# Moving the norm's latent column sums behind the fifth context panel, with three partial sums for four, and holding two weight casts behind the last pair

## The chip, the cores and the metric

The kernel runs on one core of one Trainium2 chip. The metric is the device time of one execution in microseconds (us), lower is better. The core has TensorE (PE in the profile, PEld its weight loads), VectorE (DVE), ScalarE (ACT), GpSimd (POOL) and SyncE (SP, which here only issues transfers). Each engine works through its own list of instructions in order; between engines they wait for each other's semaphores.

## The reference

Two layers of a transformer over 512 latent tokens and 256 context tokens of width 1024. In each layer the tokens are normed and modulated, mixed by attention, and then passed through a gated feed-forward part:

```
h_lat = h_lat + g_a * o_lat
h_lat = h_lat + g_f * swiglu(modulate(h_lat, sh_f, sc_f), ffn_w_gate_up[l], ffn_w_down[l])
if ctx_out:                                   # layer 0 alone
    h_ctx = h_ctx + cg_a * o_ctx
    h_ctx = h_ctx + cg_f * swiglu(modulate(h_ctx, csh_f, csc_f), ...)
...
def rms_norm(x):  return x * rsqrt(mean(x * x, axis=-1) + EPS)
def modulate(x, shift, scale):  return rms_norm(x) * (1 + scale) + shift
def swiglu(h, w_gate_up, w_down):
    g, u = split(h @ w_gate_up);  return (silu(g) * u) @ w_down
```

Layer 1 begins with `modulate` of the new `h_lat` and `h_ctx` and a projection of both (queries, keys, values). The case is about the seam between the two: the end of layer 0's feed-forward part, the norm that opens layer 1, and the first three projections.

## The kernel before

**Layout.** Activations lie transposed: 1024 features are 8 tiles (`k` or `m`, 0 to 7) of 128 partitions, tokens run along the free dimension, 512 latent columns (`LATS`) and then 256 context columns (`CTXS`). A float32 product is made of three reduced-precision matmuls: an operand is cast to a high part (`wh`, on ACT) and a low rest (`wl`, on DVE), and `mm3` multiplies high by high, high by low and low by high.

**Who sets the order.** The kernel is written in one Python program; a scheduler of the build, with a timeline of its own, then chooses the order on each engine. The call `behind(ins, *before)` adds a dependency for that scheduler alone, with no semaphore: the named instructions must stand earlier on their engine.

**The last pair of layer 0's feed-forward.** A `Pair` makes one block of 128 hidden features: `head`, `body` and `tail` each run products on PE (lines 1386 to 1388) into banks `z` and `y`. In the last step of `body`, ACT copies `z` out of PSUM (line 1436) and DVE adds `y` to it (line 1437); then `tail` goes on adding into `z`, so PE's next product waits for that ACT copy. Up to this point SP has been loading weights in order through three `wr` buffers.

**The last down projection: `output`, called by `final0`.** Its first stream makes the 8 latent panels: for each `m`, matmuls over the two remaining hidden blocks, a residual on DVE (`add_residual`, line 1227), and `norm.add`, which squares the new tile on ACT (line 383) and adds the squares up. Because `norm1` has `two=LATS`, those sums go into separate partial sums: tiles 0 to 3 on POOL, the later ones on DVE. The second stream makes the 8 context panels (256 columns each) in the same manner, with the norm of the latent columns laced in: `rest` first calls `rstd`, which sums the squares over partitions by matmuls of the partial sums against a column of ones (line 397; one per 128 tokens and partial sum), takes the square root (line 400, ACT) and the reciprocal (line 401, DVE), and spreads the result over all partitions by transposes (line 377, `spread`). Then, for each `k`, `modulate` multiplies on DVE (line 432), adds the shift and casts on ACT (line 433) and makes the low rest on DVE (line 434).

**The next weights.** While `final0` runs, `kept_w` loads and casts three weight tiles of layer 1's input projection (keys, values, first queries) at panels 3, 4 and 5: `load_w` casts on ACT (line 334, `wh`) and makes the rest on DVE (line 335, `wl`). The projection itself is at lines 765 to 767.

**PSUM.** `PG` hands out banks in a ring of s, t, s, d, t, s, d with 3 `s`, 2 `t` and 2 `d` banks; a panel waits until the residual of the panel that had its bank is done.

Of the kernel before, what the change touches and what calls it, by code (L numbers as in the profile page):

```python
# [12 lines left out]
ALU = mybir.AluOpType  # L13

P = 128
D = 1024
KT = D // P
# [52 lines left out]
BG = (0, 0, 0, 0, 0)  # L70
LATE = ((0, 1, 3, 5, 7), ()), (0,) * 4 + (1, 2, 2, 2, 1, 2, 2, 2, 1, 2, 3, 2, 1, 2, 3, 2, 0, 0), ((2,), (2,)) + ((0, 2, 4, 6),) * 3
FIRST = 2000
STEPS = ((2, 3, 4, 4), 5, 3)
HALVES = (slice(0, 256), slice(256, 512))
SWAP8 = [(i // 16) * 16 + (i % 16 + 8) % 16 for i in range(32)]
# [24 lines left out]
def hybrid_kernel(ctx: ExitStack, tc, I, out):  # L100
# [6 lines left out]
    def T(tag, shape, dt=F32):  # L107
        count[0] += 1
        if tag not in SIZES:
            return sb.tile(shape, dt, tag=tag, name=f"{tag}_{count[0]}", bufs=BUFS.get(tag, 1))  # L110
        n = int(np.prod(shape[1:]))
        t = sb.tile([P, SIZES[tag] // (2 if dt == mybir.dt.bfloat16 else 4)], dt, tag=tag, name=f"{tag}_{count[0]}",
                    bufs=BUFS[tag])[: shape[0], :n]
        if len(shape) == 3:
            t = t.rearrange("p (a b) -> p a b", a=shape[1])
        return t

    def B(dt=F32, tag="b"):
        return T(tag, [P, NT], dt)
# [12 lines left out]
    V, S, G, PE = nc.vector, nc.scalar, nc.gpsimd, nc.tensor  # L132

    def dma(o, i, eng=None):
        return (eng or nc.sync).dma_start(f(o), f(i))

    def f(ap):
        return ap.bitcast(F32) if ap.dtype == F32R else ap

    silu, marks = [], {}  # L140

    def behind(ins, *before):

        for x in before:
            tc.add_manual_dep(ins.ins, x.ins.name, mybir.DependencyInfo(mybir.DependencyClass.NoSync,
                              mybir.DependencyReason.DATA), reason="products in one run")
        return ins
# [181 lines left out]
    def load_w(src, kt, m, eng=None, tag=None, after=()):  # L329

        r = T("wr", [P, kt * m])
        dma(r, src)
        h, lo = (B(F32R, tag)[:, : kt * m] if tag else T(x, [P, kt * m], F32R) for x in ("wh", "wl"))
        behind(S.copy(h, r), *after[:1])  # L334
        behind((G if eng else V).tensor_tensor(lo, r, f(h), op=ALU.subtract), *after[1:])  # L335
        return tuple(x.rearrange("p (k m) -> p k m", k=kt) for x in (h, lo))
# [14 lines left out]
    def banks(cols, get, rows=P):  # L351

        return [(get()[:rows, : c.stop - c.start], c) for c in cols]
# [32 lines left out]
        marks["add"] = (eng or V).tensor_tensor(acc[:, :n], acc[:, :n], t[:, :n], op=ALU.add)  # L386
        return acc

    def rstd(acc, nfeat, c, r, get=PQ, tag="p"):


        n, accs = c.stop - c.start, [x for x in acc if x is not None] if type(acc) is list else [acc]
        m, d = n // P, get()
        col = T("sm", [P, 6, 2]).rearrange("p a b -> p (a b)")[:, :m]
        for j, a in enumerate(accs):
            for i in range(m):
                x = PE.matmul(d[:, i : i + 1], a[:, i * P : (i + 1) * P], ones[:, :1], start=i + j == 0,
                              stop=j == len(accs) - 1, skip_group_check=True)
                marks["sum"] = behind(x, *([marks["sum"]] if i + j else []))
        marks["root"] = S.activation(col, d[:, :m], AF.Sqrt, bias=eps, scale=1.0 / nfeat)  # L400
        marks["diag"] = V.reciprocal(col, col)
        for i in range(0, n, 512):
            w = min(512, n - i)
            d = get() if r is not None else PS("o")
            for j in range(0, w, P):
                at = (i + j) // P
                marks["spread"] = spread(d[:, j : j + P], col[:, at : at + 1].to_broadcast([P, P]))
            if r is None:
                return d
            S.copy(r[:, c.start + i : c.start + i + w], d[:, :w])  # L410
# [25 lines left out]
    class Norm:  # L436


        def __init__(self, src, use, eng=None, order=range(KT), two=None):
            self.src, self.use, self.eng, self.acc, self.order, self.two, self.marks = src, use, eng, None, order, two, {}  # L440

        def add(self, k, c):
            if c is self.two:
                self.acc = self.acc if k else [None] * 4
                i = (k > 3) + (k > 5) + (k > 6)
                self.acc[i] = square_sum(self.acc[i], self.src[k], c, eng=(G, V)[min(i, 1)])
            else:
                self.acc = square_sum(self.acc if k else None, self.src[k], c, eng=self.eng if k < KT - 1 else None)

        def rest(self, acc, c, v):  # L450
            self.marks[c.start] = own = dict(marks)
            r = Columns(rstd(acc, D, c, None, PG), c.start)
            own.update({x: marks[x] for x in ("sum", "root", "diag", "spread")})
            yield
            for k in self.order:
                self.use(k, r, c, v)
                yield
# [77 lines left out]
    def weighted(o, lanes):  # L535
# [13 lines left out]
        for n in range(max(len(m) for m in moving)):  # L549
            for i, (v, _, all_qs) in [*enumerate(lanes)][::-1]:  # L550
                if n < len(moving[i]):
                    kt, qs, t = moving[i][-1 - n]
                    c = slice((qs[0] - all_qs[0]) * P, (qs[-1] + 1 - all_qs[0]) * P)
                    with shifted(-FIRST):
                        ins = PE.matmul(o[64 * i : 64 * i + 64, c], v(kt), t, start=n == 0, stop=n == len(moving[i]) - 1)  # L555
# [205 lines left out]
    r = B(tag="nb")  # L761
# [120 lines left out]
    acc = None  # L882
    for k in range(KT):
        acc = square_sum(acc, X[k], LATS)
        behind(marks["square"], *silu)
    behind(ident_cast, marks["square"])
    _, diag = first_norm(acc, LATS)
# [8 lines left out]
    for c in range(4):  # L896
# [16 lines left out]
        if c == 3:  # L913
            _, diag = first_norm(acc, CTXS)
# [230 lines left out]
    def na_jobs():  # L1145
        for p in range(4):
            if p == 3:
                lower[0] = L3
            for x in ORDER[p]:
                beside(split_pair(int(x)) if x in "23" else {"n": latent_norms, "m": mla_prepare}[x]())  # L1150
            rate[0] = STEPS[0][p], BG[p]
            if p % 2 == 0:
# [12 lines left out]
    i = 0  # L1165
# [21 lines left out]
    def mla_jobs():  # L1187
        phase[0], lower[0] = 1, LOWER
        rate[0] = STEPS[1], BG[4]
        ready.append(latent_operands(1))  # L1190
# [43 lines left out]
    ahead, soon = {}, []  # L1234

    def kept_w(src, m):

        if 2 < m < 6:
            soon.append(load_w(I["w_in1"][(8, 9, 0)[m - 3]], KT, P))
        return ahead[m]  # L1240

    def keep_groups(k0, kc):
# [12 lines left out]
    def output(src, mov, l, comp, streams, norm, units, dst=None, keep=False, base=None, wait=0, held=()):  # L1255

        rest, kept, done = iter(()), [], []
        for i, (c, v) in enumerate(streams):
            if i and norm.two:
                next(rest)  # L1260
                own = norm.marks[streams[0][0].start]
            before = done[-1:] + ([marks["add"]] if i and norm.two else [])
            for m in range(KT):
                w = kept[m] if keep and i else keep(src, m) if callable(keep) else load_w(src(m), len(mov), P, LOE[l, comp, i], "b" if keep else None, held[m : m + 1] * 2 if i == 0 else ())
                if keep and i == 0:
                    kept.append(w)
                o = banks([c], PG)
                ins = mm3(o, w, mov)
                if i and norm.two:
                    behind(ins, *(own[x] for x in {2: ("sum",), 4: ("spread",)}.get(m, ())))  # L1270
                    before = before + [own["diag"]] if m == 2 else before
                done.append(behind(add_residual(m, o[0][0], l, comp, v, c, dst and dst[m], base and base(m, c)), *before))
                if c is TOK1:
                    G.dma_start(home[m], H[m])
                norm.add(m, c)
                if i and norm.two:
                    behind(marks["square"], own["root"])
                if m >= wait:
                    next(rest, None)
                if m in units[i]:  # L1280
                    late_step(done[-1], m < 7)
            for _ in rest:
                pass
            rest = norm.rest(norm.acc, c, v)
        for _ in rest:
            pass
# [90 lines left out]
    norm, ops, sums = combined(H, 0, 3, TOK1, TOK2)  # L1377
# [12 lines left out]
    class Pair:  # L1390
# [39 lines left out]
        def body(self):  # L1430
            self.y = PG()[:, : self.w]
            product(self.z, self.s2, self.ops["T2"])
            S.copy(self.t[:, self.c1], self.z)
            product(self.y, self.s3, self.ops["T3"], True)
            product(self.z, self.s1, self.ops["T1"])
            S.copy(self.t[:, self.c2], self.z)  # L1436
            self.done = V.tensor_tensor(self.t[:, self.c2], self.y, self.t[:, self.c2], op=ALU.add)

        def tail(self):
            product(self.z, self.s4, self.ops["22"])  # L1440
# [187 lines left out]
    lower[0] = LOWER  # L1628
    rate[0] = STEPS[2], 0
    attend(swa_jobs())  # L1630
# [7 lines left out]
    norm, ops, sums = combined(H, 1, 3, *HALVES)  # L1638
# [178 lines left out]
```

## Time and profile before

| what | value |
|---|---|
| time, median of 3 runs | 1577.79 us (1577.0, 1577.79, 1583.72) |
| the profiled execution | 1578.6 us, its span 1576.6 us |
| TensorE busy in the span | 1530.6 us (97%) |
| VectorE, ScalarE, GpSimd busy | 1174.0, 794.5, 276.0 us |
| mean granted TensorE clock | 0.992 |
| the seam, in us of the span | last pair 940 to 961, latent panels to 971, context panels and norm 971 to 986, projections from 986 |

The span reaches from the first to the last instruction; the execution's own time is 2.0 us more. A row of the timeline reads: start, duration, engine, line, operation, output<-inputs, sizes, count, and in brackets the idle time of the engine just before, with what ended it. A row of the windows gives the busy time of each engine in a stretch, then the granted TensorE clock (1.00 is full speed), the share of the DMA engines in use and GB/s. Line numbers in the profile of before are those of the kernel before; the kernel after has 1 to 4 lines more, so that line 397 is 398 there, and 1436 is 1440.

### The profile page before, as it was taken

How to read it: one execution, taken by the hardware profiler on the slowest of the kernel's cores; microseconds unless marked ns; L12 is line 12 of the kernel's file. 1: busy time of each engine (PE TensorE's matmuls, PEld its weight loads, DVE VectorE, ACT ScalarE, POOL GpSimd, SP SyncE). 2: the span in 40 equal slices, each digit the busy share in tenths (PEclk: the TensorE clock that was granted, in tenths of full speed). 3: DMA queues.
4: the chain of work that ended last, by engine and by line, in shares of the span. 5: the costliest groups of instructions: out<-in, count | busy, mean ns of one | idle time of the engine just before them, and what ended most of it. 6: DMA issues, size and time to landing. Idle time of an engine off the chain costs nothing.

```text
span 1576.6 us, 26539 instructions
## 1 busy us (share of the span) xinstructions
PE 1530.6 (97%) x10024; PEld 1375.8 (87%) x10024; DVE 1174.0 (74%) x2345; ACT 794.5 (50%) x1607; POOL 276.0 (18%) x302
## 2 busy tenths in 40 slices
PE   6999999999999999999999999999999999999998
PEld 4787778887998999999999998877889999899998
DVE  4885777685878587777858675889976778678685
ACT  4563677775465243242423334548856545454453
POOL 0144624320111101102111131470012000000001
PEclk9999999999999999999999999999999999999999
DMA  9644242004654444646466494110125123323222
GB/s 317 250 131 175 78 129 73 11 7 160 207 168 143 154 165 161 219 134 264 157 202 236 146 351 145 49 46 2 68 78 164 52 98 126 98 90 128 86 96 87
DMA packets 76463, 214.90 MB, mean 136 GB/s; under 512 B 9872, under 2 KB 16400, under 8 KB 76336
## 3 DMA queue, kind: packets, MB, share of 16 engines
q1 hardware_dynamic: 59216, 144.42, 27.6%
q0 software_dynamic: 15968, 67.24, 12.3%
q8 instruction: 78, 1.28, 0.3%
q10 hardware_dynamic: 1152, 1.57, 0.3%
q14 instruction: 49, 0.40, 0.1%
HBM read 186.97 MB, written 23.07 MB: 133 GB/s over the span
## 4 chain that ended last, share of the span: by engine, by line
PE 79%; DVE 9%; DMA 5%; ACT 3%; issue 2%; POOL 1%; SPq 0%; DVEq 0%; ACTq 0%; POOLq 0%
PE pss L1388 5%; PE pss L1387 5%; PE pss L1386 5%; PE pso L555 4%; PE pss L345 4%; PE psd L345 4%; PE pss L348 4%; PE pss L347 4%; PE psd L348 4%; PE psd L347 4%; PE pst L345 3%; PE pst L1388 3%; PE pst L1386 3%; PE pst L348 3%; PE pst L347 3%; PE pst L1387 3%
## 5 line engine op out<-in xcount | busy, mean ns | idle before, releaser
L334 ACT CAST wh<-wr 128x1024 fp32r<-128x1024 f32 (+2 forms) x148 | 115.5, 795 | 210.9 <-DMA wr<-in_w_dn_dram 42.1
L335 DVE TENSOR_TENSOR wl<-wr,wh 128x1024 fp32r<-128x1024 f32 (+2 forms) x145 | 133.9, 930 | 81.7 <-ACT wh L334 81.5
L561 ACT ACTIVATE p<-p,sm 128x512 f32<-128x512 f32 (+3 forms) x144 | 105.0, 730 | 29.0 <-DVE sm L565 27.2
L1386 PE MATMUL pss<-b,wh 128*128 128x384 f32 (+1 forms) x346 | 107.8, 312 | 0.6 <-ACT b L371 0.6
L1387 PE MATMUL pss<-b,wh 128*128 128x384 f32 (+1 forms) x346 | 108.0, 312 | 0.1
L1388 PE MATMUL pss<-b,wl 128*128 128x384 f32 (+1 forms) x346 | 107.2, 312 | 0.0
L347 PE MATMUL psd<-b,wh 128*128 128x512 f32 (+3 forms) x262 | 89.7, 343 | 0.0
L301 DVE CUSTOM_DVE_ANT_0 p<-rope,cond 128x1024 bf16<-128x1024 f32 x64 | 76.9, 1221 | 11.0 <-DMA rope<-in_mod_w_dram 10.8
L291 POOL DMA_DIRECT2D rope<-in_mod_w_dram x48 | 25.6, 533 | 318.7 <-DVE mod L301 306.0
L345 PE MATMUL psd<-b,wh 128*128 128x512 f32 (+3 forms) x222 | 80.0, 360 | 1.2 <-ACT b L474 0.9
L348 PE MATMUL psd<-b,wl 128*128 128x512 f32 (+3 forms) x222 | 78.8, 356 | 0.0
L555 PE MATMUL pso<-ph,b 128*64 128x256 f32 (+1 forms) x384 | 77.5, 361 | 0.4 <-DVE ph L500 0.2
L555 PE MATMUL pso<-pl,b 128*64 128x256 f32 (+1 forms) x384 | 77.2, 359 | 0.0
L1386 PE MATMUL pst<-b,wh 128*128 128x384 f32 (+1 forms) x226 | 70.8, 313 | 3.1 <-ACT p L1436 1.8
L1373 ACT CAST wh<-pl 128x512 fp32r<-128x512 f32 x78 | 44.9, 619 | 52.0 <-PE pss L1387 22.8
L1388 PE MATMUL pst<-b,wl 128*128 128x384 f32 (+1 forms) x226 | 70.7, 313 | 0.2 <-DVE wl L1374 0.2
L1387 PE MATMUL pst<-b,wh 128*128 128x384 f32 (+1 forms) x226 | 70.6, 312 | 0.0
L347 PE MATMUL pss<-b,wh 128*128 128x256 f32 (+3 forms) x216 | 69.3, 321 | 0.0
L1373 ACT CAST wh<-wr 128x1024 fp32r<-128x1024 f32 x39 | 41.0, 1051 | 54.4 <-PE pst L1387 14.7
L345 PE MATMUL pss<-st,wh 128*128 128x512 f32 (+2 forms) x198 | 67.2, 339 | 0.3 <-ACT wh L334 0.3
L348 PE MATMUL pss<-st,wl 128*128 128x512 f32 (+2 forms) x198 | 67.3, 340 | 0.1
L1386 PEld LDWEIGHTS pss<-b,wh 128*128 128x128 f32 x346 | 65.7, 190 | 1.1 <-ACT b L371 0.9
(624 smaller groups left out, 5387.4 us busy)
## 6 DMA issues: line engine op xcount, KB each, us to landing
wr<-in_w_gu_dram SPq DMA_DIRECT2D x88, 512.0 KB, 4.1
rope<-in_mod_w_dram POOLq DMA_DIRECT2D x48, 512.0 KB, 3.9
wr<-in_w_dn_dram SPq DMA_DIRECT2D x73, 256.0 KB, 2.9
wr<-in_w_out_dram SPq DMA_DIRECT2D x32, 512.0 KB, 4.2
p<-home POOLq DMA_DIRECT2D x40, 384.0 KB, 5.5
home<-p POOLq DMA_DIRECT2D x40, 384.0 KB, 5.4
wr<-in_w_in_dram SPq DMA_DIRECT2D x21, 512.0 KB, 3.8
nb<-in_nb_dram SPq DMA_DIRECT2D x16, 384.0 KB, 3.3
```

Of the source, the lines that this page charges most:

```text
L301: behind(V.tensor_tensor_reduce(out=T("p", [P, D], mybir.dt.bfloat16), in0=w, in1=cond[:, v, :], op0=ALU.mult, op1=ALU.add, scale=1.0, sca ...
L334: behind(S.copy(h, r), *after[:1])
L335: behind((G if eng else V).tensor_tensor(lo, r, f(h), op=ALU.subtract), *after[1:])
L345: ins = PE.matmul(o, wh[:, k], mh[:, c], start=first and k == 0, stop=False)
L347: PE.matmul(o, wh[:, k], ml[:, c], start=False, stop=False)
L348: PE.matmul(o, wl[:, k], mh[:, c], start=False, stop=last and k == n - 1)
L555: ins = PE.matmul(o[64 * i : 64 * i + 64, c], v(kt), t, start=n == 0, stop=n == len(moving[i]) - 1)
L561: S.activation(p[:, c], p[:, c], AF.Exp, bias=nm, scale=-1.0, accum_out=dn)
L1373: S.copy(h, t)
L1386: PE.matmul(o, wh, xh, start=first and k == 0, stop=False, skip_group_check=not first)
L1387: PE.matmul(o, wh, xl, start=False, stop=False, skip_group_check=not first)
L1388: PE.matmul(o, wl, xh, start=False, stop=k == 3, skip_group_check=not first)
```

## The change

Three edits. `norm1` keeps three partial sums of the latent squares and not four: tile 7 is added to the sum of tile 6 on DVE. The column sums, which stood behind the first context panel, are written in ahead of the sixth (`m == 5`) and held behind the fifth panel's first matmul; the sixth panel is held behind the sums, the seventh (`m == 6`) behind the spread, and the squares of the context tiles 5 to 7 behind the root. And of the three next weight tiles, the second and third are cast (and their rests made) only behind the last DVE step of the last pair's `body`, which `marks["middle"]` names.

```diff
+SUMS = 5, 6
...
-    def rstd(acc, nfeat, c, r, get=PQ, tag="p"):
+    def rstd(acc, nfeat, c, r, get=PQ, tag="p", after=()):
...
-                marks["sum"] = behind(x, *([marks["sum"]] if i + j else []))
+                marks["sum"] = behind(x, *([marks["sum"]] if i + j else after))
...
-                self.acc = self.acc if k else [None] * 4
-                i = (k > 3) + (k > 5) + (k > 6)
+                self.acc = self.acc if k else [None] * 3
+                i = (k > 3) + (k > 5)
...
-            r = Columns(rstd(acc, D, c, None, PG), c.start)
+            r = Columns(rstd(acc, D, c, None, PG, after=self.hold), c.start)
...
-            soon.append(load_w(I["w_in1"][(8, 9, 0)[m - 3]], KT, P))
+            soon.append(load_w(I["w_in1"][(8, 9, 0)[m - 3]], KT, P, after=(marks["middle"],) * (m > 3)))
...
-            if i and norm.two:
-                next(rest)
-                own = norm.marks[streams[0][0].start]
+            late = i and norm.two
...
+                if late and m == SUMS[0]:
+                    norm.hold = ins,
+                    next(rest)
+                    norm.hold, own = (), norm.marks[streams[0][0].start]
+                    before = before + [own["diag"]]
                 o = banks([c], PG)
                 ins = mm3(o, w, mov)
-                if i and norm.two:
-                    behind(ins, *(own[x] for x in {2: ("sum",), 4: ("spread",)}.get(m, ())))
-                    before = before + [own["diag"]] if m == 2 else before
+                if late and m in SUMS:
+                    behind(ins, own[("sum", "spread")[SUMS.index(m)]])
...
-                if i and norm.two:
+                if late and m >= SUMS[0]:
                     behind(marks["square"], own["root"])
-                if m >= wait:
+                if m >= (SUMS[0] if late else wait):
...
-            self.done = V.tensor_tensor(self.t[:, self.c2], self.y, self.t[:, self.c2], op=ALU.add)
+            self.done = marks["middle"] = V.tensor_tensor(self.t[:, self.c2], self.y, self.t[:, self.c2], op=ALU.add)
```

**TensorE, the context panels.** A panel is six matmuls of 128x256; `st` are the two hidden blocks, `nb` and `st_97..` the weights, `ones` by `p_9864`, `p_9919` and so on the column sums of the partial sums, `ident_r` by `sm` the spread. Before, from the last matmul of the first context panel on:

```order
L348 MATMUL psd_9983<-st_9645,nb_9744 128x256
L397 MATMUL pss_9958<-ones_93,p_9864 128x1 x4
L397 MATMUL pss_9958<-ones_93,p_9919 128x1 x4
L397 MATMUL pss_9958<-ones_93,p_9946 128x1 x4
L397 MATMUL pss_9958<-ones_93,p_9956 128x1 x4
L345 MATMUL pss_9993<-st_9540,nb_9743 128x256
...
L348 MATMUL pst_10061<-st_9540,st_9750 128x256
L377 MATMUL pso_9978<-ident_r_86,sm_9959 128x128 x4
L345 MATMUL psd_10044<-st_9540,st_9749 128x256
```

After, from the last matmul of the fifth context panel on:

```order
L349 MATMUL pss_10002<-st_9645,st_9750 128x256
L398 MATMUL psd_10013<-ones_93,p_9864 128x1 x4
L398 MATMUL psd_10013<-ones_93,p_9919 128x1 x4
L398 MATMUL psd_10013<-ones_93,p_9946 128x1 x4
L346 MATMUL pst_10034<-st_9540,st_9749 128x256
...
L349 MATMUL psd_10068<-st_9645,st_9756 128x256
L378 MATMUL pso_10029<-ident_r_86,sm_10014 128x128 x4
L346 MATMUL pss_10051<-st_9540,st_9755 128x256
...
L767 MATMUL pst_10189<-b_10045,wh_9890 128x512
```

The sums move from behind panel 1 of 8 to behind panel 5 and fall from 16 matmuls to 12; between sums and spread stood three and a half panels (21 matmuls) and now stand two (12), and between the spread and the first projection three and a half and now one.

**ScalarE, the last pair.** `p_9680<-pst_9681` is the copy of the last pair's bank `z`, the `CAST` of `wh` those of the next weights. Before:

```order
L1373 CAST st_9755<-wr_9754 128x512
L334 CAST wh_9907<-wr_9905 128x1024
L1436 COPY p_9680<-pst_9681 128x384
L1373 CAST st_9540<-p_9574 128x384
L334 CAST wh_9923<-wr_9921 128x1024
L1441 ACTIVATE p_9679<-pst_9681 128x384
```

After:

```order
L1377 CAST st_9755<-wr_9754 128x512
L1440 COPY p_9680<-pst_9681 128x384
L1377 CAST st_9540<-p_9574 128x384
L335 CAST wh_9907<-wr_9905 128x1024
L335 CAST wh_9923<-wr_9921 128x1024
L1445 ACTIVATE p_9679<-pst_9681 128x384
```

The copy that PE waits for now stands ahead of the cast of the values' weights; the cast of the queries' weights keeps its place ahead of the silu.

**ScalarE, the root.** `p<-b ... 128x256` are squares of context tiles, the `ACT_TABLE_LOAD` belongs to the square root. Before:

```order
L383 ACTIVATE p_9956<-b_9839 128x512
L400 ACT_TABLE_LOAD
L400 ACTIVATE sm_9959<-pss_9958,eps_91 128x4
L383 ACTIVATE p_9991<-b_9832 128x256
L383 ACTIVATE p_10001<-b_9833 128x256
```

After:

```order
L384 ACTIVATE p_9956<-b_9839 128x512
L384 ACTIVATE p_9967<-b_9832 128x256
L384 ACTIVATE p_9977<-b_9833 128x256
L384 ACTIVATE p_9988<-b_9834 128x256
L384 ACTIVATE p_9999<-b_9835 128x256
L384 ACTIVATE p_10010<-b_9836 128x256
L401 ACT_TABLE_LOAD
L401 ACTIVATE sm_10014<-psd_10013,eps_91 128x4
L384 ACTIVATE p_10042<-b_9837 128x256
```

Five context squares now stand ahead of the table load and the root; behind it comes the sixth.

On DVE the order changes in the same way: the fourth partial sum becomes one more addition (`p_9946<-p_9946,p_9956`) ahead of the first context residual, and the reciprocal stands behind the fifth context residual and not behind the first. On SP, the transfers `parked` (the latent result to memory, held behind the root for the scheduler) now stand behind the load of a mask that used to follow them. Outside the seam only the first scores of layer 1's attention stand in a slightly other order on PE and DVE.

More of the change, by code (lines that the diff above doesn't have):

```diff
@@ L440, in __init__ @@
             self.src, self.use, self.eng, self.acc, self.order, self.two, self.marks = src, use, eng, None, order, two, {}
+            self.hold = ()
         def add(self, k, c):
             if c is self.two:
-                self.acc = self.acc if k else [None] * 4
-                i = (k > 3) + (k > 5) + (k > 6)
+                self.acc = self.acc if k else [None] * 3
+                i = (k > 3) + (k > 5)
                 self.acc[i] = square_sum(self.acc[i], self.src[k], c, eng=(G, V)[min(i, 1)])
```

## The prediction

> **What bounds the kernel.** I read the page first, then the windows around the seam, then what PE waited for there, then the timeline of each engine in it.
>
> ```profile
> span 1576.6 us, 26539 instructions
> PE 79%; DVE 9%; DMA 5%; ACT 3%; issue 2%; POOL 1%; SPq 0%; DVEq 0%; ACTq 0%; POOLq 0%
> ```
>
> The chain that ended last runs through PE for 79% of the span, so time is won where PE stands still or runs slowly. The windows by stage (last pair, latent panels, context panels and norm, projections, then the way into attention) show where that is:
>
> ```profile
> 940.00:955.00 15.00, 14.06 (x82) 13.74 (x80) 7.66 (x13) 6.97 (x12) 2.14 (x4) 1.00 0.71 251
> 955.00:971.00 16.00, 15.19 (x72) 13.30 (x73) 9.71 (x15) 6.56 (x12) 1.56 (x2) 1.00 0.45 160
> 971.00:986.00 15.00, 13.53 (x88) 13.19 (x86) 7.54 (x14) 7.03 (x14) 4.50 (x5) 0.77 0.33 120
> 986.00:1004.00 18.00, 17.57 (x80) 14.02 (x79) 14.19 (x29) 8.10 (x17) 2.40 (x3) 1.00 0.01 1
> 1004.00:1014.00 10.00, 10.00 (x70) 9.22 (x69) 7.33 (x12) 4.32 (x9) 7.96 (x6) 1.00 0.15 52
> 1014.00:1032.00 18.00, 18.00 (x87) 15.10 (x86) 17.52 (x24) 11.57 (x17) 13.33 (x8) 1.00 0.33 117
> ```
>
> From 971 to 986 PE is idle for 1.5 us and its granted clock is 0.77; from 1004 to 1032 it never stops, so what PE wins before 1004 has nothing there that would swallow it. What PE waited for between 940 and 1070:
>
> ```profile
> PE pst L1386 <- ACT p L1436: 1.8, 1, 1.8
> PE pss L397 <- POOL p L386: 1.5, 1, 1.5
> PE pss L755 <- DVE sm L565: 1.1, 1, 1.1
> ...
> PE pst L766 <- DVE b L434: 0.4, 1, 0.4
> ```
>
> The change aims at the first two; the fourth it can only worsen.
>
> **The last pair.** PE's two rows and ACT's three:
>
> ```profile
> 953.73 0.34 PE L1388 MATMUL pst<-b,wl 128*128 128x384 f32 x1
> 955.82 0.44 PE L1386 MATMUL pst<-b,wh 128*128 128x384 f32 x1 [1.75 <-ACT p L1436]
> ```
>
> ```profile
> 954.34 1.04 ACT L334 CAST wh<-wr 128x1024 fp32r<-128x1024 f32 x1 [1.35 <-DMA wr<-in_w_in_dram]
> 955.29 0.47 ACT L1436 COPY p<-pst 128x384 f32<-128x384 f32 x1
> ...
> 958.10 1.05 ACT L334 CAST wh<-wr 128x1024 fp32r<-128x1024 f32 x1 [1.92 <-PE pst L1387]
> ```
>
> PE's product ends at 954.07. ACT is then casting a weight for which it had stood idle 1.35 us, and copies only at 955.29. With the copy ahead, it starts at about 954.1, so PE restarts at 954.65 in place of 955.82: -1.2 us. Bounds: 0 if ACT is late anyhow, -1.75 if the whole wait went. I take -1.2, since every part of it is in these rows. What now queues behind the copy: the values' cast (about 955.1 to 956.1), then the queries' cast, which may stay at 958.1 if it is its own transfer and not PE that ends last, and behind it the silu that stood at 959. A silu that comes no earlier is harmless: PE reads that pair's products in its second half of the latent panels, some 5 us later. The two casts and their DVE rests are read by the projections, from 985.7; that cover is 26 us long, and the cost is nothing. `middle` adds no semaphore, and the order shows that the edit does what it says.
>
> **The sums.** PE around them:
>
> ```profile
> 971.67 0.28 PE L348 MATMUL psd<-st,nb 128*128 128x256 f32 x1
> 973.42 5.63 PE L397 MATMUL pss<-ones,p 128*128 128x1 f32 x32 [1.48 <-POOL p L386]
> ...
> 979.49 0.42 PE L348 MATMUL pss<-st,nb 128*128 128x256 f32 x1
> 979.70 0.41 PE L345 MATMUL pss<-st,nb 128*128 128x256 f32 x1
> ...
> 981.82 0.28 PE L347 MATMUL pss<-st,st 128*128 128x256 f32 x1
> 981.93 0.28 PE L348 MATMUL pss<-st,st 128*128 128x256 f32 x1
> ```
>
> First, the wait of 1.48 us. After, four more panels stand ahead of the sums: 4 x 6 x 0.12 (the step from 981.82 to 981.93) = 2.9 us, so PE reaches them at about 974.7 by the old clock, when POOL has long ended. -1.5 us.
>
> Second, the sums themselves: 16 matmuls in two passes are 32 rows in 5.63 us; 12 will be 24. The price of a row depends on the clock:
>
> ```profile
> 974.00:974.50 0.50, 0.50 (x7) 0.50 (x6) 0.31 (x1) 0.50 (x1) 0.00 (x0) 1.00 0.99 377
> 974.50:975.00 0.50, 0.50 (x6) 0.50 (x5) 0.00 (x0) 0.08 (x1) 0.00 (x0) 0.94 1.02 385
> 975.00:975.50 0.50, 0.50 (x4) 0.50 (x4) 0.00 (x0) 0.00 (x0) 0.00 (x0) 0.50 0.72 270
> ...
> 981.50:982.00 0.50, 0.50 (x5) 0.50 (x5) 0.14 (x1) 0.07 (x1) 0.35 (x1) 0.73 0.00 0
> ```
>
> The grant falls to half at about 974.97 and comes back at 981.8: most of the sums and the twelve matmuls behind them run at half clock. At full clock the same kind of row is priced by the final norm:
>
> ```profile
> 1556.57 1.84 PE L1658 MATMUL psd<-ones,p 128*128 128x1 f32 x16
> ```
>
> 0.115 us each, so 24 cost 2.8 us: -2.9 us. Bounds: at the old mean of 0.176 they cost 4.2 (-1.4); at 0.115 it is -2.9.
>
> Third, the twelve slow matmuls at 0.21 (979.49 to 979.70) in place of 0.12: -1.1 us if the clock holds, 0 if not.
>
> Does it hold? Before 974.97 PE had streamed real columns only until 971.9; 1.5 us of idling and 1.5 of one-column rows followed, and the clock fell. The 1.75 us idle at 954 did not make it fall (1.00 in both windows there). After, the run of one-column rows is 2.8 us with full panels on both sides: between the two, nearer to the one that fell. [...]
>
> By rows alone: let the clock be judged over stretches of 3.4 us (half of the dip from 974.97 to 981.8), and let a fall need 2.4 us without real columns in one of them (halfway between 1.75 and 3.0). A run of 2.8 us then meets it at (0.6 + 2 x 0.4) / 3.4, some 4 in 10 positions. I take "holds" for the sum and the fall as a rival.
>
> **What the move adds.** The rows of the chain from sums to the first projection, ACT and DVE, and the spread and first projections on PE:
>
> ```profile
> 973.30 1.28 ACT L400 ACT_TABLE_LOAD   x1
> 979.09 0.26 ACT L400 ACTIVATE sm<-pss,eps 128x4 f32<-128x4 f32 x1 [4.51 <-PE pss L397]
> ...
> 984.18 1.38 ACT L433 ACTIVATE b<-p,mod 128x512 fp32r<-128x512 f32 x2 [0.64 <-DVE p L432]
> 985.47 0.71 ACT L383 ACTIVATE p<-b 128x256 f32<-128x256 f32 x2
> ```
>
> ```profile
> 972.47 1.45 DVE L386 TENSOR_TENSOR p<-p,p 128x512 f32<-128x512 f32 x1
> 973.84 0.47 DVE L1227 SCALAR_TENSOR_TENSOR b<-psd,mod,b 128x256 f32<-128x256 f32 x1
> 979.39 0.18 DVE L401 RECIPROCAL sm<-sm 128x4 f32<-128x4 f32 x1 [5.08 <-ACT sm L400]
> ...
> 983.40 1.41 DVE L432 SCALAR_TENSOR_TENSOR p<-b,mod,pso 128x512 f32<-128x512 f32 x2 [0.31 <-PE pso L377]
> ```
>
> ```profile
> 982.76 0.60 PE L377 MATMUL pso<-ident_r,sm 128*128 128x128 f32 x4
> ...
> 985.71 0.40 PE L765 MATMUL pst<-b,wh 128*128 128x512 f32 x1
> ...
> 988.41 0.50 PE L766 MATMUL pst<-b,wh 128*128 128x512 f32 x1 [0.43 <-DVE b L434]
> ```
>
> The new DVE addition (0.7 to 1.45 us by the row at 972.47) starts at 973.84 and ends by 975.3; PE needs it after 16 rows of sums, at 976.5. Hidden.
>
> The root now stands behind five context squares and the table load. The context residuals start behind that addition, say at 974.6, and step by 0.4; the fifth ends at 976.6, its square at 977.05, the table load (1.28) at 978.35. The sums end at 974.7 + 2.8 = 977.5, so the load, once hidden, is late by 0.9 us; root and reciprocal bring the column to 978.85. PE has two panels (1.4 us) to pass that time, to 978.9. Cost 0, with no margin: every further tenth costs a tenth. Bounds 0 and +1 (the addition at 1.45, and one more residual late).
>
> From the spread on: DVE's first product starts 0.64 us after the spread does, ACT's cast 1.42 after, and takes 0.7. So PE can project 2.2 us after the spread began and has until then 0.36 of spread and one panel of 0.72: idle 1.1. The low rest (0.74 on DVE) and the second tile, in the new DVE order, cost it another 0.3 and 0.5. Before, three and a half panels covered this, and the waits were 0.43 and 0.12. So +1.4 us; bounds +0.5 (the first idle alone, less the old waits) and +3.
>
> SP: the `parked` transfers queue behind the mask load, which waits for PE's last read of `nb` in the third context panel (973.2). They start 5 us later; nothing reads them before attention is over. POOL has the same rows in the same order. In the first scores of attention PE's order shifts by some rows near the wait of 1.1 us on L565: 0, bounds -1 and +1.
>
> **The sum**, against the profiled execution of 1578.6 us: -1.2 (pair) -1.5 (wait) -2.9 (sums) -1.1 (slow panels) +0 (root) +1.4 (first projection) = -5.3, so 1573.3 us. That execution stands 0.8 above the median of 1577.79, so the gain against the median is 4.5 us, or 0.3%. A change of 0.5%, 7.9 us, is about what a measurement of this kernel can tell from no change: I expect a real gain too small for that.
>
> **The rivals.**
>
> The clock still falls behind the sums. For it: the row at 975.00, and a run of 2.8 us at almost full loads. Then some 3.4 us of panels run at half speed, costing 1.7 less the 0.2 that the idling before the projection absorbs: +1.5, 1574.8 us. Chance 0.30.
>
> The wait moves instead of going: DVE does residuals, modulation and rests in one line, and PE idles 4.5 us before and in the first projections, not 1.9. For it: DVE is busy 14.19 of 18 us there; against it: a tile takes two DVE operations of 0.7 us, and PE waited only 0.43 for them. 1576 us, chance 0.13.
>
> Slower than before: the root. Five squares, each behind a residual behind a panel, stand before it on one in-order engine. If POOL holds the `p` buffers that these squares need, or DVE's addition drags, ACT is late and PE has no further panel to run. Each us is lost in full, and it decides from 5.3 us on; PE would then idle long enough for the clock to fall as well, some 1580 us. Against it: POOL's latent additions end by 973.4. Chance 0.05.
>
> More than I count: attention's first wait of 1.1 us goes too and the copy wins all its 1.75: about 1571.5. Chance 0.10.
>
> **The numbers.** The forecast, clock held, has 0.42: 1573.3 us. The range of 1570.8 to 1577.0 takes in the fall, the larger gain and most of the moved wait. Faster by over 0.5% needs the large gain and more: 0.05; slower by that much: 0.02; the rest, 0.93, is within.
>
> **What would show it.** The copy of `z` starting within 0.1 us of PE's last row of that product; no idle ahead of the ones; 24 rows in 2.8 us with the clock at 1.00; the spread right behind the second panel; an idle of about 1 us ahead of the first L767 row. Wrong would prove a clock of 0.50 behind the sums, a root later than 1 us after them, or waits of over 3 us in the first three tiles of the projection.

## The result, and the profile after

| kernel | median us | runs | ratio to the kernel before, 95% interval |
|---|---|---|---|
| before | 1578.26 (1575.6 to 1586.73) | 17 | |
| after | 1573.63 (1570.5 to 1581.96) | 17 | 0.9968 (0.9956 to 0.9979) |
| after, in a later comparison (before there 1579.78) | 1573.64 (1570.18 to 1575.83) | 6 | 0.9955 (0.9939 to 0.9971) |

A gain of 4.6 us, near the forecast of 1573.3 us and inside its range. The prediction held a gain of 0.3% for too small to tell from none; over 17 runs each it can be told, since the interval ends below 1. The profiled execution of after, however, took 1578.6 us, as long as that of before. So the place of the change must be read by itself. First, what PE waited for between 935 and 1070 us (us in total, times, longest):

```profile
PE pss L757 <- DVE sm L567: 1.2, 1, 1.2
PE pst L767 <- ACT b L434: 1.1, 2, 0.9
PE pst L1392 <- DVE wl L1378: 0.8, 1, 0.8
...
PE pst L1390 <- ACT p L1440: 0.6, 1, 0.6
```

The wait for POOL ahead of the sums is gone, the one for the copy of `z` (line 1440 now) has shrunk from 1.8 to 0.6, and the first projections wait 1.1. The third row stands in the pair before, ahead of everything that the change touches. The timeline of the pair, PE and then ACT:

```profile
957.77 0.34 PE L1392 MATMUL pst<-b,wl 128*128 128x384 f32 x1
958.73 0.44 PE L1390 MATMUL pst<-b,wh 128*128 128x384 f32 x1 [0.62 <-ACT p L1440]
...
958.20 0.48 ACT L1440 COPY p<-pst 128x384 f32<-128x384 f32 x1 [1.17 <-PE pst L1392]
...
958.99 1.05 ACT L335 CAST wh<-wr 128x1024 fp32r<-128x1024 f32 x1
961.21 1.05 ACT L335 CAST wh<-wr 128x1024 fp32r<-128x1024 f32 x1 [1.17 <-DMA wr<-in_w_in_dram]
```

ACT copies 0.09 us behind PE's product, and the casts follow. The sums and what comes behind them, on PE and on ACT and DVE:

```profile
977.56 2.73 PE L398 MATMUL psd<-ones,p 128*128 128x1 f32 x24
...
981.54 0.28 PE L349 MATMUL psd<-st,st 128*128 128x256 f32 x1
981.77 0.65 PE L378 MATMUL pso<-ident_r,sm 128*128 128x128 f32 x4
...
984.01 0.50 PE L767 MATMUL pst<-b,wh 128*128 128x512 f32 x1 [0.88 <-ACT b L434]
...
986.22 0.50 PE L767 MATMUL pst<-b,wh 128*128 128x512 f32 x1 [0.22 <-ACT b L434]
```

```profile
979.95 1.28 ACT L401 ACT_TABLE_LOAD   x1
981.24 0.26 ACT L401 ACTIVATE sm<-psd,eps 128x4 f32<-128x4 f32 x1
...
981.54 0.18 DVE L402 RECIPROCAL sm<-sm 128x4 f32<-128x4 f32 x1 [2.12 <-ACT sm L401]
```

No idle ahead of the ones, 24 rows in 2.73 us, the root's reciprocal ready at 981.72 while the second panel's last matmul runs, and a new wait of 0.88 us, then one of 0.22. The windows of that stretch (the granted clock stands behind the five engines):

```profile
977.50:980.30 2.80, 2.80 (x27) 2.80 (x27) 1.92 (x5) 2.34 (x6) 1.39 (x2) 1.00 0.93 342
980.30:982.30 2.00, 2.00 (x17) 1.85 (x18) 0.76 (x3) 1.37 (x3) 1.53 (x3) 1.00 1.02 379
```

The clock held at 1.00. To compare kernels whatever happens elsewhere, I take the **seam**: from the start of PE's last row of the product that ACT copies (953.73 before, 957.77 after) to the start of ACT's first rope copy out of `psd` (1007.12 and 1005.40). It took 53.4 us before and 47.6 after, a gain of 5.8 us.

Where did that execution lose it? Against the same ACT instructions of before it lay 0.9 us late at 700 us, 1.8 at 840, 3.4 from 850 on and 4.0 at 950; behind the seam it was 1.7 early, and level again from 1075. Two of the losses, some 1.6 us each, show in its windows:

```profile
842.15:845.56 3.41, 1.54 (x10) 1.22 (x9) 3.41 (x7) 1.28 (x2) 0.28 (x1) 1.00 0.10 42
845.56:848.97 3.41, 3.41 (x12) 3.41 (x11) 3.37 (x6) 0.00 (x0) 1.01 (x3) 0.50 0.66 188
...
1053.77:1057.18 3.41, 1.77 (x12) 1.06 (x10) 3.35 (x10) 1.83 (x4) 3.33 (x3) 1.00 0.00 0
1057.18:1060.60 3.42, 3.42 (x18) 2.44 (x20) 3.35 (x10) 1.04 (x3) 0.09 (x1) 0.50 0.00 0
```

Twice PE stood still for half of a stretch of 3.41 us, and in the next 3.41 us its clock was granted at half. In the profile of before the clock stayed at 1.00 at both places, with waits of nearly the same length (1.39 and 1.1 us for 1.87 and 1.23). The first place lies ahead of the change. At the second, in attention, the clock fell in 1 of the 3 profiles with the sums in their old place (the hold alone) and in 4 of the 9 with the sums moved: too few to tell a difference, so the fall there isn't charged to the change, but it isn't shown to be free of it. What the falls went with, the experiments show.

### The profile page after: what moved, and what is told of

Its sections match the earlier page's. It is cut to its first block, busy times and chain, and to the rows that moved or that the text cites. A ratio compares the mean times of both kernels' runs of the same rounds, so it can differ in the third digit from the quotient of the medians.

```text
span 1576.8 us, 26525 instructions
## 1 busy us (share of the span) xinstructions
PE 1529.3 (97%) x10016; PEld 1372.7 (87%) x10016; DVE 1174.8 (75%) x2346; ACT 796.1 (50%) x1607; POOL 276.3 (18%) x302
## 4 chain that ended last, share of the span: by engine, by line
PE 77%; DVE 10%; DMA 6%; ACT 3%; issue 2%; POOL 0%; SPq 0%; DVEq 0%; ACTq 0%; POOLq 0%
PE pso L557 5%; PE pss L1392 5%; PE pss L1391 5%; PE pss L1390 4%; PE psd L346 4%; PE psd L349 4%; PE psd L348 4%; PE pss L346 4%; PE pss L349 4%; PE pss L348 3%; PE pst L1392 3%; PE pst L1390 3%; PE pst L1391 3%; PE pst L346 3%; PE pst L348 3%; PE pst L349 3%
```

## The experiments

All seams, in one table (measured from the start of PE's row as above, also where an expectation speaks of its end): idle time of PE in the pair, idle ahead of and within the sums, rows of one column and their time, length of the half clock that began in or behind them, idle of PE ahead of the spread and in the first two tiles of the projection. Every ratio below is to the kernel before as timed beside that run, whose median was 1579.24 to 1579.78 us.

| kernel | pair | sums | rows, us | half clock | spread; projection | seam |
|---|---|---|---|---|---|---|
| before | 1.75 | 1.48 | 32, 5.63 | 6.83 | 0; 0.43 | 53.4 |
| after, first profile | 0.62 | 0 | 24, 2.73 | none | 0; 0.88, 0.22 | 47.6 |
| after, second | 0.62 | 0 | 24, 3.06 | 6.83 | 0; 0.31, 0.21 | 49.6 |
| after, third | 0.62 | 0 | 24, 2.93 | 3.41 | 0; 0.88, 0.22 | 49.0 |
| hold of the casts alone | 0.62 | 1.49 | 32, 5.74 | 10.24 | 0; 0.45 | 53.6 |
| sums alone | 1.89 | 0 | 24, 2.73 | 3.41 | 0; 0.32, 0.18, 0.22 | 49.7 |
| four partial sums, moved | 0.62 | 0 | 32, 3.63 | 3.41 | 0; 0.32, 0.84 | 49.6 |
| three partial sums, in place | 1.97 | 1.47 | 16 and 8, 1.95 and 1.70 | 6.83 | 0; 0.17, 0.56 | 52.9 |
| two partial sums, early | 0.62 | 0.71 | 16 | none | 0; 0.95, 0.23 | 47.3 |
| two partial sums, moved | 0.62 | 0 | 16, 1.99 | none | 0.50; 0.95, 0.23 | 47.2 |
| fixed order | 0.62 | 0 | 16, 1.99 | none | 0.18; 0.25, 0.82 | 46.8 |
| fixed order, early | 0.62 | 0.71 | 16 | none | 0; 0, 0.39, 0.31 | 46.8 |

**The hold of the casts alone.** Before, with `after=(marks["middle"],) * (m > 3)` in `kept_w` and the mark.

> The old kernel with the second half of the change alone: the last two weight casts held behind the pair's middle, the sums where they were. What is compared in the trace here and below is the seam: from the end of PE's last row of T1 in the last pair to the start of ACT's first copy out of the projected keys (rope, b<-psd), 53.4 us in the old kernel's trace and 47.6 in the new one's. Theory (the terms add up): the wait ahead of the next product falls from 1.75 us to about 0.6, the wait for POOL ahead of the sums stays at 1.5 or grows by what POOL does not gain, the clock still falls behind the sums, and the seam takes 52.2 us; time 1.2 us below the old kernel's. Rival (the copy only moves the wait): PE comes to the sums 1.2 us earlier and waits there 2.7 us for POOL, whose additions hang on the same squares; seam 53.4, time unchanged.

1577.84 us, ratio 0.9984 (0.9959 to 1.0009). The wait in the pair fell to 0.62 us and the wait for POOL stayed at 1.49, so the rival's mechanism is out: POOL gained what PE gained. But the seam is no shorter, because the clock stayed at half for 10.24 us here and not 6.83:

```profile
978.10:979.50 1.40, 1.35 (x12) 1.36 (x13) 0.93 (x2) 1.19 (x1) 0.00 (x0) 1.00 0.96 364
979.50:983.00 3.50, 3.50 (x19) 3.50 (x18) 0.00 (x0) 0.00 (x0) 0.00 (x0) 0.51 0.03 11
983.00:986.40 3.40, 3.40 (x17) 3.40 (x17) 0.66 (x2) 0.98 (x3) 0.00 (x0) 0.50 0.00 0
986.40:989.80 3.40, 3.40 (x18) 3.40 (x17) 1.30 (x3) 0.83 (x3) 2.21 (x3) 0.50 0.19 58
```

The 1.1 us won ahead of the sums went into 0.9 more from the sums to the spread and 0.7 more from there to the projection.

**The sums alone.** After, without that argument.

> The new kernel without the hold of the two casts: the sums moved and three for four, the casts as in the old kernel. Theory (the terms add up): the wait of 1.75 us in the pair is back, everything from the sums on stands as in the new kernel (24 rows in 2.7 to 2.8 us, clock 1.00), seam 48.8 us, time 4.1 us below the old kernel's. Rival (the early copy also makes room for the sums): without it ACT and POOL come later and PE waits ahead of the moved sums as well, seam 50 us or more, and the clock falls.

1574.09 us, ratio 0.9966 (0.9943 to 0.9989). The wait of 1.89 us is back, PE waits nowhere ahead of the sums: the rival is out in that, the parts don't lean on each other. But the clock fell behind the sums, for 3.41 us, with the same 24 rows in the same 2.73 us behind which it had held in the first profile of after. The seam is 0.9 us over the 48.8 expected; I put that down to the fall.

**Four partial sums at the new place.** After, with `[None] * 4` and `i = (k > 3) + (k > 5) + (k > 6)`.

> The new kernel with four partial sums in place of three: 32 rows at the new place. Rows cost 0.115 us at full clock, so 3.7 us. Theory (the clock falls when a window of 3.41 us has under about a third of its time in streaming matmuls): the run now covers up to the whole of a window and the clock falls in some 7 executions of 10; where it falls, the rows cost 0.17 to 0.2 us and twelve to twenty matmuls behind them run at half speed, seam 50 to 51 us; where it does not, 48.5. Rival (only idle time makes the clock fall, and rows of one column count as work): the clock stays at 1.00 and the seam is 48.5, time 0.9 us above the new kernel's.

1574.41 us, ratio 0.9971 (0.9953 to 0.9989); seam 49.6. The fall came, for 3.41 us, so the rival is out, but it came behind the rows, which still ran at full clock (3.63 us); 0.9 us of the 2.0 over after's best seam are the eight rows.

**Three partial sums at the old place.** Before, with `[None] * 3` and `i = (k > 3) + (k > 5)`.

> The old kernel with three partial sums in place of four and nothing moved: 24 rows, still behind the wait for POOL. Theory (idling and one-column rows together make the clock fall): 1.5 us of waiting and 2.8 to 4.2 us of rows are over a window, the clock falls, rows cost 0.15 to 0.18 us, seam 51.9 to 52.4, time 1 to 1.5 us below the old kernel's. Rival (fewer rows alone keep the clock): clock 1.00, 24 rows in 2.8 us, seam 49.5, time 4 us below the old kernel's, and the move then brought only the wait.

1577.37 us, ratio 0.9987 (0.9973 to 1.0001). The rival is out: the clock fell for 6.83 us. The seam's gain of 0.5 us is under the theory's 1 to 1.5, as the third partial sum's eight rows stood nine matmuls behind the others and ran wholly at half clock, 1.70 us for eight. Fewer rows alone bring little, and in the time nothing that can be told from no change; it is the move that brings the gain.

**The clock by itself.** Bursts of 512-column matmuls, each 0.227 us, with eight interruptions between them, 30 times over:

```
PLAN = (0, 8), (0, 12), (0, 16), (2, 0), (4, 0), (6, 0), (2, 6), (2, 12)
...
        for stop, few in PLAN:
            to = idle(stop) if stop else mov      # a chain of ACT copies that PE waits for
            ...
            rows(few)                             # matmuls into one column, two rows each
            burst(BURST + (k * 5 + stop + few) % 16, to)
```

> A kernel of its own, which computes nothing of the reference: 30 cycles of eight interruptions, each between bursts of 45 to 60 matmuls of 512 columns (10 to 14 us): 16, 24 and 32 rows of one column (1.85, 2.8, 3.7 us), idling behind 2, 4 and 6 ACT copies (I estimate 1.5, 2.6 and 3.7 us), idling behind 2 copies followed by 12 rows (2.9 us) or 24 rows (4.3 us). Theory (the clock is granted by windows of 3.41 us that run free of the kernel, and a window with under a third of its time in streamed columns costs the next one; idling and one-column rows are alike): falls need 2.3 us in one window, so 0 of 30 behind 16 rows, 14 behind 24, 22 behind 32, 0, 12 and 22 behind the three idlings, 15 behind 2.9 us of both, 27 behind 4.3. Rival (only idling counts, a row of one column is work): no falls behind any number of rows, and none behind both, since 1.5 us of idling alone is too short; some behind 6 copies.

| interruption | us without a full matmul | clock fell |
|---|---|---|
| 16 rows of one column | 1.70 | 0 of 30 |
| 24 rows | 2.60 | 18 of 30 |
| 32 rows | 3.49 | 26 of 30 |
| idle behind 2, 4, 6 copies | 1.54, 2.84, 4.14 | 0, 22, 30 of 30 |
| idle, then 12 rows; idle, then 24 rows | 3.01; 5.28 | 18; 30 of 30 |

The rival is out: the clock fell behind rows of one column (18 of 30 behind 2.60 us) as it did behind idling (22 of 30 behind 2.84). Where falls came, the theory's counts were 3 to 10 too low: its border of 2.3 us is above what the windows below show, and the idle stretches came out longer than estimated. Every fall lasted 3.41 us or a multiple (but for the one that the program's end cuts off), and all lie on one grid of that step, so I laid windows of 3.41 us on that grid and took the interrupted time in each window that ran at full clock. For rows, the longest time that did not lead to a fall is 1.94 us and the shortest that did is 1.92; for idling the two are 2.09 and 1.89, for both together 2.04 and 2.14. So in this run, for idling and one-column rows alike, the change from holding to falling lies between 1.89 and 2.14 us without streamed columns in one of these windows.

Counted the other way round, by the 512-column matmuls that start in a window: with up to 5 of them 130 of 131 windows at full clock led to a fall, with 6 or 7 it was 14 of 66, with 8 or more 0 of 755. The same holds while the clock is at half: behind up to 6 started matmuls the clock stayed at half in 43 of 43 windows, behind 7 in 2 of 25, behind 8 or 9 in 0 of 121. So in this run a fall went on for a further window where the window at half clock, too, streamed little. By this count the fall at 845.56 in the first profile of after is a border case: eight matmuls of 384 columns start in the window ahead of it, as many columns as six of 512.

Two of the 24-row interruptions, one that held and one that fell:

```profile
36.10:39.50 3.40, 3.40 (x16) 2.81 (x16) 0.00 (x0) 0.00 (x0) 0.00 (x0) 1.00 0.00 0
39.50:42.10 2.60, 2.60 (x25) 2.56 (x24) 0.00 (x0) 0.00 (x0) 0.00 (x0) 1.00 0.00 0
42.10:45.50 3.40, 3.40 (x17) 2.79 (x17) 0.00 (x0) 0.00 (x0) 0.00 (x0) 1.00 0.00 0
293.18:296.59 3.41, 3.41 (x29) 3.27 (x28) 0.00 (x0) 0.00 (x0) 0.00 (x0) 1.00 0.00 0
296.59:300.00 3.41, 3.41 (x10) 2.63 (x9) 0.00 (x0) 0.00 (x0) 0.00 (x0) 0.50 0.02 5
```

The border of two windows lies at 40.6 in the second row and splits its run into 1.05 and 1.55 us; in the fourth row the whole run lies inside one window, and the fifth shows 10 matmuls where the third has 17. PE shows as busy through all of them, for 2.60 of 2.60 us in the second row and 3.41 of 3.41 in the fourth: the busy share doesn't tell the interruption that held from the one that fell.

**After, a second and a third profile.** The kernel unchanged.

> The new kernel unchanged, for a second profile of its seam. Theory (position of the window decides): some 4 in 10 executions have the clock fall behind the 24 rows; with the fall the seam (53.4 us in the old kernel's trace, 47.6 in the new one's first) takes 48.5 to 49, without it 47.6. Rival (the order of the new kernel protects the clock): 47.6 each time.

> The new kernel unchanged, timed beside the two versions on the same chip, with a third profile of its seam. Theory (window position): seam 47.6 us without a fall behind the sums (in some 4 to 5 of 10 executions, by 18 falls of 30 behind 24 rows in the clock study) and 48.5 to 49.6 with it; time 1573.5 to 1574.5 us. Rival: a fall in none of the further profiles, and the one seen was a disturbance.

The clock fell in both. The second profile's windows:

```profile
968.10:970.40 2.30, 2.30 (x23) 2.30 (x22) 1.94 (x5) 1.84 (x5) 0.88 (x2) 1.00 0.91 331
970.40:973.80 3.40, 3.40 (x17) 3.40 (x17) 0.66 (x2) 2.11 (x4) 2.04 (x3) 0.50 1.02 380
973.80:977.20 3.40, 3.09 (x13) 2.54 (x12) 2.26 (x4) 1.16 (x3) 0.73 (x1) 0.50 0.15 58
```

With the run of the sums alone, three of the four profiles that have 24 rows at the new place fell, which fits the 18 of 30 of the study; the rival (protected by the order, or a disturbance) is out. A fall took 1.4 us (3.41 us at half clock) or 2.0 (6.83) of the seam here, and in the runs of the sums alone and of four partial sums about 1.

Which of them fell goes with the position. In each profile all changes of the clock lie on one grid of 3.413 us, to 0.01 us; I carried that grid on to the sums also where nothing fell there. The stretch from the first row of the sums to the next panel, with any wait within it, is split by them as follows (the last four versions are told of below):

| profile | us without streamed columns | us in either window | clock |
|---|---|---|---|
| after, first | 2.59 | 1.12 and 1.47 | held |
| after, second | 2.92 | 2.24 and 0.68 | fell |
| after, third | 2.79 | 2.39 and 0.40 | fell |
| sums alone | 2.59 | 0.25 and 2.34 | fell |
| four partial sums, moved | 3.48 | 0.97 and 2.51 | fell |
| two partial sums, moved | 1.86 | 1.86 and 0 | held |
| two partial sums, early | 2.57 | 2.02 and 0.55 | held |
| fixed order | 1.85 | 0.89 and 0.96 | held |
| fixed order, early | 2.58 | 0.72 and 1.86 | held |

The clock fell behind every window with 2.24 us or more and behind none with up to 2.02, which fits the study's 1.89 to 2.14. The second profile's execution took 1570.1 us all the same, and the first's, which held, 1578.6: what happens elsewhere weighs as much.

**Versions meant to be faster.** Two partial sums make 16 rows, a run of 1.85 and 1.86 us in the kernel, just under the 1.89 behind which the study's shortest fall came; first at the new place, all else equal:

> The new kernel with two partial sums for three, nothing else changed: 16 rows. Theory: 0.9 us less in rows, but the root still stands behind the table load that comes behind the fifth square, so PE waits that time ahead of the spread instead: the spread starts where it did, seam 47.4 to 47.6; the clock does not fall, so the mean time is 0.4 to 0.6 us below the new kernel's (4 in 10 of 1.2 us). Rival (DVE's third addition in a row is late): PE waits within the sums, seam 48 to 48.5.

1575.41 us, ratio 0.9976 (0.9959 to 0.9994), seam 47.2, no fall. The theory is right in the wait: PE now waits 0.50 us ahead of the spread, for the root behind its table load. The 0.4 to 0.6 us that it forecast for the time against after can't be seen (after has 0.9968, 0.9956 to 0.9979). Then with that load taken early and the sums a panel ahead:

```diff
-SUMS = 5, 6
+SUMS = 4, 5
...
+        behind(S.activation(T("part", [P, 1]), eps, AF.Sqrt), marks["silu"])
```

> A version meant to beat the new kernel: two partial sums (16 rows), sums one panel earlier (before the fifth context panel's successor no longer, but before the fifth), and the table load for the root taken out of the chain by a small root on ACT behind the last silu of the pair. Theory (rows, cover and window as in the new kernel): 1.85 us of rows, no fall of the clock ever, the wait ahead of the first projection (0.9 us) covered by one panel more; seam 46.0 us, time 1.5 to 2.5 us below the new kernel's, the larger part from executions in which the new kernel's clock falls. Rival (POOL and DVE are not done one panel earlier): PE waits 0.5 to 1.5 us ahead of or within the sums, seam 47 to 48, no gain.

1574.19 us, ratio 0.9975 (0.996 to 0.999), seam 47.3: the rival's value, in part by its cause (0.71 us of waiting for DVE's addition within the sums), in part by one that neither had. Only one panel is tied to the spread in the code; the scheduler had put the last two ahead of it, so that one panel still stood behind it and the wait ahead of the projection stayed at 0.95. Nor is the clock safe here, as the theory had it: with the wait within the sums PE goes 2.57 us without streamed columns, as long as with 24 rows, and 2.02 of them fell into one window; that it held here and in the last version (2.58 us, 0.72 and 1.86) I put down to luck of position. The next two hold all later panels behind the spread, with the sums at the new place and a panel ahead:

```diff
-                if late and m in SUMS:
-                    behind(ins, own[("sum", "spread")[SUMS.index(m)]])
+                if late and m >= SUMS[0]:
+                    behind(ins, own["spread" if m >= SUMS[1] else "sum"])
```

> A version meant to beat the new kernel: sums behind the fifth context panel as there, but two partial sums (16 rows), the table load for the root ahead of time behind the last silu of the pair, and every panel after the sixth held behind the spread, so that two panels and not one stand between the spread and the first projection. Theory (terms read from the runs so far): rows 1.9 us in place of 2.7, the 0.5 us that PE waited for the root with two partial sums gone, the wait ahead of the first projection down from 0.95 to about 0.3 us; seam 46.1 us, never a fall of the clock, since a window then streams over 0.40 of its time, where in the clock study a fall needed 0.38 or less. Time 1572 to 1573 us, 1 to 2 us below the new kernel's. Rival (DVE decides: the two residuals that now come behind the spread stand ahead of the products on it): the wait stays at 0.9 us, seam 46.8.

> The same version with the sums one panel earlier, behind the fourth, and three panels behind the spread. Theory: PE waits 0.7 us within the sums for DVE's third addition, as in the run with two early partial sums, and has no wait ahead of the first projection; seam 46.3 us, time as the version before within 0.5 us. Rival (the wait moves on to the second projected tile, for DVE's low rest): seam 46.8 to 47.

1572.74 us, ratio 0.9958 (0.9942 to 0.9974), and 1573.82 us, ratio 0.9958 (0.9942 to 0.9973). Both seams are 46.8: the rivals were right (in the first the wait is split, 0.25 and 0.82, and not 0.9 at one place). The 0.38 of the first theory is not the study's limit as counted above, where the shortest fall came behind 1.89 of 3.41 us, which leaves 0.45; here no window at the sums had more than 0.96 us and the clock held. In the first of the two PE:

```profile
969.41 1.99 PE L398 MATMUL psd<-ones,p 128*128 128x1 f32 x16
972.39 0.65 PE L378 MATMUL pso<-ident_r,sm 128*128 128x128 f32 x4 [0.18 <-DVE sm L402]
974.71 0.50 PE L767 MATMUL pst<-b,wh 128*128 128x512 f32 x1 [0.25 <-ACT b L434]
976.25 0.50 PE L768 MATMUL pst<-b,wh 128*128 128x512 f32 x1 [0.82 <-DVE b L435]
```

The wait moved from ACT's cast to DVE's low rest, which stands behind two residuals. This version's seam is 0.8 us shorter than the best of after and 2.2 to 2.8 shorter than the two that fell, but beside after on the same chip (1573.64 us) its time can't be told apart.

## Why the prediction was right, step by step

- **The copy ahead of the cast, -1.2.** 1.75 to 0.62 us of idling: -1.13. Right, shown alone by the hold of the casts (0.62) and its absence (1.89). That is PE's wait; in the time of the whole kernel this part isn't shown, the sums alone having the ratio 0.9966 and after 0.9968.
- **The wait for POOL, -1.5.** Gone in all runs with the sums moved, 1.47 to 1.49 in all others. Right.
- **24 rows at full clock, -2.9.** 5.63 to 2.73 us. Right where the clock held; in the two profiles of after where it fell 2.93 and 3.06, because the fall came in the rows' last 0.8 us.
- **Twelve slow matmuls, -1.1.** Right where the clock held; where it fell, matmuls behind the rows stepped by 0.21 us again (second profile, 971.46 to 971.67, against 0.12 at full clock).
- **The root, 0 with no margin.** Right: the column was there at 981.72, as the second panel's last matmul ran, and with 8 rows less PE waited 0.50 for it.
- **The first projections, +1.4.** Oversized: 0.88 and 0.22 against 0.43 and 0.12 before, so +0.55. The first idle was near the 1.1 counted; the further 0.3 and 0.5 us that I added for the first tile's rest and the second tile came to 0.22 together, since PE has six rows on the first tile to pass the time with.
- **The chances.** This is the step that was mis-sized the most. I set the border of a fall halfway between an idling that held (1.75 us) and a stretch that fell (3.0), at 2.4 us, and gave the held clock 0.42 and the fall 0.30. The study has it at some 2.0 (1.89 to 2.14). That the clock holds, which the sum takes for the usual case, no run shows: it held behind 12 of the study's 30 runs of 24 rows and in 1 of the 4 profiles with 24 rows at the new place. By the same working, with 2.0, I estimate that a run of 2.6 us meets it at (0.8 + 2 x 0.6) / 3.41, 6 in 10. So the likelier case was the rival's (1574.8), and the median of 1573.63 lies between the two forecasts: the seam gains 5.8 us with the clock held (5.3 forecast) and 3.8 and 4.4 with a fall (3.8 forecast). That the median came within 0.3 us of the forecast is in part luck: the projections cost some 0.9 us less than counted, and the fall, which the sum leaves out, came in more than half of the cases (18 of 30 in the study, 3 of the 4 profiles) and took 1.4 to 2.0 us in the profiles of after. An estimate with these chances, 0.4 x 5.8 + 0.6 x 4.1, gives 4.8 us for the 4.6 measured.
- The other rivals: the waits of the first projections never reached 4.5 us, the root was never late enough to cost, attention's first wait stayed (1.2 for 1.1).

The prediction took stretches of 3.4 us as half of one dip. In the profiles all stretches at half clock that the kernel's end doesn't cut off were 3.41, 6.83 or 10.24 us long; in that of before 3.41 from 22.65 and from 213.80, 6.83 from 179.66 and from 974.97. Idle time wasn't needed for a fall: behind 24 rows with none at all the clock fell in 18 of the study's 30.

## What to carry to other kernels

Count for PE not idle time but time without streamed columns: here a wait and the one-column sums beside it added up. In the study the clock fell 0 times of 30 behind 1.54 and 1.70 us of such time, 18 to 26 times behind 2.60 to 3.49 and 30 times behind 4.14 and 5.28; at the moved sums, in nine profiles of the kernel and its variants, it fell behind every 3.41 us window with 2.24 us or more of it and behind none with up to 2.02. Between the extremes the result went with the position, so one profile showed one draw, and a change of a few us is judged by its own stretch over several profiles and by the median of many runs. When a step is laced into others, tie down every step that must follow it, not just the next: what is left free, the scheduler may put ahead.

## What the runs showed of the hardware that I had not expected

- A PE that is busy throughout by the profile, loading weights and streaming one column each, lost its clock as an idle one did: 18 of 30 behind 2.60 us of rows, 22 of 30 behind 2.84 us of idling, 0 of 30 behind 1.70 and 1.54.
- The half clock came late in the sums or behind them: at the new place the 24 rows took 2.73 to 3.06 us, almost the full clock's time, and panels and the spread after them stood at 0.50 for 3.41 or 6.83 us where it fell.
- Waits that differ by a few tenths stood ahead of different clocks in the next 3.41 us: behind 1.39 us of idling (before) the clock held at 1.00, behind 1.87 at the same place (after) it was 0.50, and the first profile of after lost about 3 of the seam's 5.8 us around two such windows elsewhere.
